# A decoder trunk's opening re-ordered: first w_mod tile loaded before x, seven bias units multiplied before the second K-tile, indicators of five of them made on GpSimd

## The chip, the cores and the metric

The kernel runs on one NeuronCore of a Trainium2 chip. The metric is the device time of one execution in microseconds (us), as the median of several runs. Engines are named as the profile names them: PE (TensorE, matmul), PEld (its weight loads), DVE (VectorE), ACT (ScalarE), POOL (GpSimd) and SP (SyncE, which here only issues DMAs).

## The reference, cut to what matters

```python
for l in range(DEPTH):                                  # DEPTH = 2, x is 512 x 2048, f32
    mod = silu(c) @ w_mod[l] + b_mod[l]                 # 2048 -> 3 * 2048
    shift, scale, gate = split(mod, 3)
    h = rmsnorm(x, norm_gain[l]) * (1 + scale) + shift
    proj = h @ w_in[l]                                  # 2048 -> 7504
    ...
    # group A: sparse attention; its logits get a bias from the positions alone:
    bias = rel_bias[t5_bucket(pos[q] - pos[k])]         # 32 buckets, 8 heads
    # group B: retention with rotary embedding
    x = x + gate * (concat([y_a, y_b]) @ w_out[l])
```

## The kernel before

Activations are kept transposed: model columns on partitions, the 512 tokens along the free axis. A K-tile is 128 of the 2048 model columns; there are 16, numbered 0 to 15 here. Every large product is made in three f32r passes (h-high by w-high, h-low by w-high, h-high by w-low), so each chunk of a weight (`wf`, from DRAM) is split into `wh` by ACT (L261) and `wl` by DVE (L268). A ring of three buffers each holds `wf`, `wh` and `wl`; SP issues the load of a chunk once the buffer of the chunk three before it is free.

`start()` is the opening. It is written out by hand, and each engine runs its part in the written order. It does, in this order:

- loads the constants `cst`, then the 16 K-tiles of x (256 KB each), then `w_mod`, laid out as one 128x2048 tile (1 MB) for each K-tile and each of scale and shift. Tile b=0 and b=1 make K-tile 0 ready, b=2 and 3 K-tile 1, and so on. The first four tiles come as two halves of 512 KB. Up to four tiles' loads stand ahead of their use;
- PE runs matmuls of zeros (`warm`) until there is work;
- `cb`, silu(c) spread over all partitions, is made by PE and copied by DVE; ACT squares each K-tile of x (L554), DVE adds the squares (`ssq`, L559), PE sums them over partitions (`row_sums`, L502), and `rstd_col` makes 1/rms and spreads it (`prb`, L484);
- `mod0_add()` multiplies one `w_mod` tile (or half) by `cb` and sums it on DVE (L349): 1.2 us for a half, 2.3 us for a tile. When the second tile of a K-tile is done, ACT makes h-high (L524) and DVE h-low (L530);
- `PLAN` lists the early chunks in the order in which PE takes them. `("S", i, kk)` is chunk i of the 336 columns of keys, values and indexer keys, `("E", i, a, b, kk)` group i of 256 columns over K-tiles a to b; a last number takes one K-tile of a two-tile chunk. Between these pieces `start()` puts a `mod0_add()` for every 4 units of PE cost, and one piece of the bias table for every 6.

The bias table is built in 32 units (j, q), each for 16 query rows against the first 128*(j+1) keys. A unit has four indicator tiles `ind` (128 thresholds against positions; ACT, Sign, L736), twelve matmuls with 32 output partitions each (L750, bf16), one evacuation `bt` (ACT, L755) and a store to DRAM, from which layer code reads it after 540 us. The units begin when K-tile 2 is ready, narrow ones first. PSUM has four banks under the tag `px` (units, E groups, broadcasts, warm-up) and four under `pj` (S and the rest).

The names `md`, `mp` are results of `mod0_add`, `hv` an f32 copy of h of which h-low is the rest, `part` the kept sums of an E group.

## Time and profile before

| | us |
|---|---|
| median of 3 runs (1915.17 to 1915.78) | 1915.41 |
| the profiled execution | 1916.6 |
| its span, first to last instruction | 1914.7 |
| PE busy in the span | 1888.6 (99%) |
| DVE busy | 1306.9 (68%) |
| ACT busy | 817.5 (43%) |
| POOL busy | 39.1 (2%) |

The span is what the trace shows; the profiled execution took 1.9 us more than it. PE's busy time counts the warm-up matmuls and matmuls at a lowered clock too. The page's row of the granted clock is 7 tenths in the first of 40 slices and 9 (90% or more) in the other 39.

### The profile page before, as it was taken

The page shows a single profiled execution, that of the slowest core. Times are in us where ns is not written, and L with a number is a line of the kernel's source. Part 1 is how long each engine was busy: PE and PEld are TensorE (multiplying, and loading weights), DVE is VectorE, ACT ScalarE, POOL GpSimd, SP SyncE. Part 2 cuts the span into 40 slices and gives each one's busy share as a digit, 9 for nine tenths or more (in the row PEclk, how much of TensorE's full clock was granted, in tenths as well). Part 3 has the DMA queues.
Part 4 walks back from the last instruction along what each step waited for, and adds up shares of the span by engine and source line. Part 5 has one row for each costly group of instructions (what it writes and reads, how often), then busy time and mean ns, then how long its engine had stood idle before and what let it go on. Part 6 is the DMA issues. An engine that isn't in the chain of part 4 may idle for free.

```text
span 1914.7 us, 24729 instructions
## 1 busy us (share of the span) xinstructions
PE 1888.6 (99%) x9136; PEld 1561.8 (82%) x9136; DVE 1306.9 (68%) x2261; ACT 817.5 (43%) x1498; POOL 39.1 (2%) x144
## 2 busy tenths in 40 slices
PE   7999999999999999999999999999999999999999
PEld 6777777888888888888888887888888888888887
DVE  7995699887867846877665579557775776564232
ACT  4666692355446522422233441244444563233111
POOL 0000000000000000100000000000000000000000
PEclk7999999999999999999999999999999999999999
DMA  9996233333352556689853223333324254553442
GB/s 369 334 307 214 88 91 108 99 110 100 121 176 89 176 176 231 235 286 309 307 162 110 78 77 99 107 92 110 99 88 125 85 190 140 180 184 121 143 139 103
DMA packets 166473, 304.44 MB, mean 159 GB/s; under 512 B 16336, under 2 KB 72144, under 8 KB 162768
## 3 DMA queue, kind: packets, MB, share of 16 engines
q1 hardware_dynamic: 166352, 302.86, 48.4%
q8 instruction: 72, 1.18, 0.2%
q14 instruction: 49, 0.40, 0.1%
HBM read 289.18 MB, written 13.63 MB: 158 GB/s over the span
## 4 chain that ended last, share of the span: by engine, by line
PE 83%; DVE 9%; ACT 4%; issue 2%; DMA 1%; SPq 0%; DVEq 0%; ACTq 0%
PE pj L322 20%; PE pj L324 20%; PE pj L323 20%; PE pj L328 5%; PE pj L329 5%; PE pj L330 5%; DVE wl L268 2%; DVE mw L349 1%; DVE iacc L872 1%; DVE iacc L857 1%; DVE m L871 1%; PE ptr L168 1%; PE plg L1068 1%; PE psc L949 1%; PE plg L1070 1%
## 5 line engine op out<-in xcount | busy, mean ns | idle before, releaser
L268 DVE TENSOR_TENSOR wl<-wf,wh 128x1024 fp32r<-128x1024 f32 (+3 forms) x309 | 366.5, 1187 | 436.8 <-ACT wh L261 423.7
L261 ACT ACTIVATE wh<-wf 128x1024 fp32r<-128x1024 f32 (+3 forms) x309 | 319.0, 1032 | 808.7 <-PE pj L323 591.0
L322 PE MATMUL pj<-h,wh 128*128 128x512 f32 x1280 | 502.6, 393 | 3.3 <-ACT h L524 2.5
L323 PE MATMUL pj<-h,wh 128*128 128x512 f32 x1280 | 500.9, 391 | 2.2 <-DVE h L530 2.2
L324 PE MATMUL pj<-h,wl 128*128 128x512 f32 x1280 | 500.5, 391 | 0.9 <-DVE wl L268 0.9
L322 PEld LDWEIGHTS pj<-h,wh 128*128 128x128 f32 x1280 | 240.7, 188 | 56.2 <-issue 2.9
L324 PEld LDWEIGHTS pj<-h,wl 128*128 128x128 f32 x1280 | 241.0, 188 | 52.3 <-DVE wl L268 2.7
L323 PEld LDWEIGHTS pj<-h,wh 128*128 128x128 f32 x1280 | 241.0, 188 | 51.6 <-DVE h L530 2.9
L328 PE MATMUL pj<-wh,h 128*128 128x512 f32 (+1 forms) x640 | 241.0, 377 | 2.9 <-DVE vm L887 2.6
L329 PE MATMUL pj<-wl,h 128*128 128x512 f32 (+1 forms) x640 | 240.2, 376 | 0.9 <-DVE wl L268 0.9
L330 PE MATMUL pj<-wh,h 128*128 128x512 f32 (+1 forms) x640 | 239.4, 376 | 0.0
L322 PE MATMUL pj<-y,wh 128*128 128x512 f32 x512 | 199.2, 389 | 0.0
L324 PE MATMUL pj<-y,wl 128*128 128x512 f32 x512 | 199.2, 389 | 0.0
L323 PE MATMUL pj<-y,wh 128*128 128x512 f32 x512 | 199.2, 389 | 0.0
L328 PEld LDWEIGHTS pj<-wh,h 128*128 128x128 f32 x640 | 120.2, 188 | 26.0 <-ACT wh L261 3.4
L329 PEld LDWEIGHTS pj<-wl,h 128*128 128x128 f32 x640 | 120.2, 188 | 20.6 <-DVE wl L268 1.4
L330 PEld LDWEIGHTS pj<-wh,h 128*128 128x128 f32 x640 | 119.7, 188 | 20.7 <-issue 0.4
L324 PEld LDWEIGHTS pj<-y,wl 128*128 128x128 f32 x512 | 96.1, 188 | 20.2
L322 PEld LDWEIGHTS pj<-y,wh 128*128 128x128 f32 x512 | 96.1, 188 | 20.1
L323 PEld LDWEIGHTS pj<-y,wh 128*128 128x128 f32 x512 | 96.1, 188 | 19.8
L349 DVE CUSTOM_DVE_ANT_0 mw<-mw,cb 128x1024 f32<-128x1024 f32 (+1 forms) x64 | 93.1, 1454 | 10.0 <-POOL mp L348 5.6
L349 DVE CUSTOM_DVE_ANT_0 mw<-mw,cb,mp 128x1024 f32<-128x1024 f32 x68 | 88.4, 1299 | 14.6 <-POOL md L348 7.6
(442 smaller groups left out, 2133.7 us busy)
## 6 DMA issues: line engine op xcount, KB each, us to landing
wf<-in_w_in_dram SPq DMA_DIRECT2D x155, 512.0 KB, 3.5
mw<-in_wmod_dram SPq DMA_DIRECT2D x136, 512.0 KB, 5.6
wf<-in_w_in_dram SPq DMA_DIRECT2D x136, 256.0 KB, 3.0
wf<-in_w_out_dram SPq DMA_DIRECT2D x64, 512.0 KB, 4.1
mw<-in_wmod_dram SPq DMA_DIRECT2D x28, 1024.0 KB, 7.8
dec<-in_decay_dram SPq DMA_DIRECT2D x32, 256.0 KB, 4.0
xT<-in_xt_dram SPq DMA_DIRECT2D x16, 256.0 KB, 5.3
bias<-bias_d SPq DMA_DIRECT2D x16, 256.0 KB, 4.3
```

Of the source, the lines that this page charges most:

```text
L168: nc.tensor.transpose(o, i, idn)
L261: act(h[:, :n], wf[i][:, :n], AF.Copy)
L268: tt(lo[:, :n], wf.pop(i)[:, :n], f(whl[i][:, :n]), op=OP.subtract)
L322: mm(g.ps[n], wh[:, o:o + P], ah, start=s0, stop=False)
L323: mm(g.ps[n], wh[:, o:o + P], al, start=False, stop=False)
L324: mm(g.ps[n], wl[:, o:o + P], ah, start=False, stop=s1)
L328: mm(q, ah[:, n * P:(n + 1) * P], wh[:, o:o + g.N], start=s0, stop=False)
L329: mm(q, ah[:, n * P:(n + 1) * P], wl[:, o:o + g.N], start=False, stop=False)
L330: mm(q, al[:, n * P:(n + 1) * P], wh[:, o:o + g.N], start=False, stop=s1)
L349: nc.vector.tensor_tensor_reduce(w[:, lo:hi], w[:, lo:hi], cb[:, lo:hi], scale=ng(l, k, 1) if q == 1 else 1.0, scalar=init, op0=OP.mult, o ...
L857: stt(a[:, :w], r[:, :w], L["WI"][:, c0:c0 + 1], a[:, :w], op0=OP.mult, op1=OP.add)
L871: nc.vector.max(m8, a[:, :w])
```

## The change

- SP loads the four halves of `w_mod` tiles 0 and 1 before x. `cst` is cut in two: 144 columns (identity, c) on SP's queue, the rest and the positions on ACT's queue.
- K-tile 0's four `mod0_add` stand among the squares of x instead of behind them. `cb` is copied by ACT and DVE in turns. K-tile 0's h is made by `make_h` in halves of 256 tokens straight from the PSUM of `prb`.
- The positions' conversion, the thresholds and doubled copies of the three bf16 parts of the bias differences (`be`, for indicators of +-0.5 rather than +-1) are made on POOL at the start.
- Units now run from the widest (j = 3, 512 keys) to the narrowest. Seven wide ones are multiplied in the opening: one after the tenth square, one after `prb`, five between K-tile 0's and K-tile 1's matmuls. `EU` says who makes their indicators: 1 is POOL (five units, 20 instructions of 128x512), 0 is ACT (two).
- `PLAN` takes S before E, and E group 1 whole after K-tile 1. `warm` numbers change.

```diff
-PLAN = [("E", 0, 0, 2, 0), ("E", 1, 0, 2, 0), ("S", 0, 0), ("E", 0, 0, 2, 1), ("E", 1, 0, 2, 1), ("S", 0, 1),
+PLAN = [("S", 0, 0), ("E", 0, 0, 2, 0), ("S", 0, 1), ("E", 0, 0, 2, 1), ("E", 1, 0, 2),
...
-WA, WS, WR = 36, 4, 8
+WA, WS, WL, WR = 24, 4, 20, 8
+
+EU = [1, 1, 0, 1, 0, 1, 1]
+EUK = (9,)
...
-    dma(cst, cst_d)
+    posi = gen.tile([P, T], I32, name="posi", tag="g")
+    dma(cst[:, :C_CAUS], cst_d[:, :C_CAUS])
+    adma(cst[:, C_CAUS:], cst_d[:, C_CAUS:])
+    adma(posi, bass.AP(tensor=positions.tensor, offset=positions.offset, ap=[[0, P], [1, T]]))
...
+        mod0_loads(4)
         for k in range(KT):
             load_x(k)
-        mod0_loads(2)
         ahead(1, 0)
-        mod0_loads(4)
+        mod0_loads(6)
...
+        get_ind(2)
         pss = psum.tile([P, T], F32, name="prs", tag="pj")
-        ssq, col = G("ssq"), 0
+        ssq, col, u = G("ssq"), 0, 0
+        mod0_add()
         for k in range(KT):
...
-            if k == 11:
+            if k < 3:
                 mod0_add()
+            if k in EUK:
+                flush()
+                begin(u)
+                u += 1
+        flush()
         col = row_sums(pss, ssq, col)
-        mod0_add()
-        rstd_col(pss, col, lambda: ahead(3, 0, 1))
         warm(WR)
-        mod0_add()
-        warm(WR, mpart["t"])
-        mod0_add()
-        xr0 = make_xr(0)
+        rstd_col(pss, col, lambda: ahead(3, 0, 1), "pj")
+        ahead(3, 1)
+        begin(u)
+        u += 1
+        make_h(0, 0, X[0], state["prb"])
         copy_rstd()
-        warm(WR // 2, mod_col(0, 0, 0))
+        ahead(3, 2)
+        flush()
+        get_ind(u + 3)
...
+            if kend == 2:
+                for u in range(u, len(EU)):
+                    begin(u)
+                    flush(1)
+                flush()
+                u = len(EU)
...
+    UNITS = [(j, q) for j in reversed(range(NB)) for q in range(8)]
...
+                if pool:
+                    nc.gpsimd.tensor_scalar(v, tab["pos"][:, :w], tab["pt"][:, col:col + 1], 0.5, op0=OP.is_lt, op1=OP.subtract)
+                else:
+                    act(v, tab["pos"][:, :w], AF.Sign, bias=tab["pt"][:, col:col + 1], scale=-1.0)
```

Three places in the engines' programs show what moves. First DVE, around the last sums of squares and 1/rms. An ISA row with `mw` is the product of one `mod0_add`, the ISA row behind it reads its sum out; `mb` is the bias of the modulation. Before, from K-tile 0's first product to its last:

```order
L349 ISA mw,mp<-mw,cb 128x1024
L349 ISA mp 128x1
L559 TENSOR_TENSOR ssq<-ssq,sq 128x512 x3
L349 ISA mw,md_88<-mw,cb,mp 128x1024
L349 ISA md_88 128x1
L474 TENSOR_REDUCE rcol<-prs 128x4
L478 RECIPROCAL rcol<-rcol 128x4
L349 ISA mw,mp<-mw,cb,cst 128x1024
L349 ISA mp 128x1
L349 ISA mw,md_88<-mw,cb,mp,cst 128x1024
L349 ISA md_88 128x1
L353 TENSOR_TENSOR md_88<-md_88,mb_90 128x2
```

After, from K-tile 0's third product to its h:

```order
L354 ISA mw,mp<-mw,cb,cst 128x1024
L354 ISA mp 128x1
L591 TENSOR_TENSOR ssq<-ssq,sq 128x512
L354 ISA mw,md_90<-mw,cb,mp,cst 128x1024
L354 ISA md_90 128x1
L358 TENSOR_TENSOR md_90<-md_90,mb_92 128x2
L591 TENSOR_TENSOR ssq<-ssq,sq 128x512 x9
L480 TENSOR_REDUCE rcol<-prs 128x4
L484 RECIPROCAL rcol<-rcol 128x4
L273 TENSOR_TENSOR wl<-wf,wh 128x672
L441 SCALAR_TENSOR_TENSOR u<-xT,md_90,prb 128x256 x2
L444 SCALAR_TENSOR_TENSOR h<-u,md_90,h 128x256 x2
```

K-tile 0's products now stand in front of the last nine sums of squares; between the sums and h only 1/rms and one split of weights are left.

Second ACT, from the square root in `rstd_col` to K-tile 1's h (the last `h` row of each piece). Before:

```order
L475 ACTIVATE rcol<-rcol,eps 128x4
L261 ACTIVATE wh<-wf 128x512
L490 ACTIVATE rstd<-prb 128x256 x2
L524 ACTIVATE h<-xT,md_88 128x512
L261 ACTIVATE wh<-wf 128x512
L261 ACTIVATE wh<-wf 128x672
L524 ACTIVATE h<-xT,md_88 128x512
```

After:

```order
L481 ACTIVATE rcol<-rcol,eps 128x4
L266 ACTIVATE wh<-wf 128x672
L442 ACTIVATE h<-u,md_90 128x256 x2
L496 ACTIVATE rstd<-prb 128x256 x2
L266 ACTIVATE wh<-wf 128x512
L794 ACTIVATE bt<-pb,top 128x512
L778 ACTIVATE ind<-pos,pt 128x512 x8
L530 ACTIVATE h<-xT,md_90 128x512
L794 ACTIVATE bt<-pb,top 128x512 x5
```

Eight indicators stand in front of K-tile 1's h, and five evacuations of units behind it.

Third SP, from the third chunk's load to the loads of groups E4 and E5 (`128x3x128`). Before:

```order
L253 DMA wf<-in_w_in_dram 128x2x256 x2
L669 DMA posi<-in_positions_dram 128x512
L381 DMA mw_408<-in_wmod_dram 128x2048
L381 DMA mw_435<-in_wmod_dram 128x2048
L381 DMA mw_441<-in_wmod_dram 128x2048
L381 DMA mw<-in_wmod_dram 128x2048
L253 DMA wf<-in_w_in_dram 128x3x128 x4
```

After:

```order
L258 DMA wf<-in_w_in_dram 128x2x256 x2
L797 DMA bias_d<-bt 128x512 x2
L386 DMA mw_480<-in_wmod_dram 128x2048
L386 DMA mw_487<-in_wmod_dram 128x2048
L386 DMA mw_493<-in_wmod_dram 128x2048
L386 DMA mw<-in_wmod_dram 128x2048
L797 DMA bias_d<-bt 128x512 x5
L258 DMA wf<-in_w_in_dram 128x3x128 x2
```

Seven stores of 256 KB now stand ahead of E4's weights.

## Rows read from the trace of the kernel before

**Rows 1.** The page: span, and busy time of each engine.

```profile
span 1914.7 us, 24729 instructions
PE 1888.6 (99%) x9136; PEld 1561.8 (82%) x9136; DVE 1306.9 (68%) x2261; ACT 817.5 (43%) x1498; POOL 39.1 (2%) x144
```

**Rows 2.** Busy time by stretch: the stretch, its length, busy us of PE, PEld, DVE, ACT and POOL (with the count of instructions), granted PE clock as a share, mean busy share of the DMA engines, GB/s.

```profile
0.00:28.47 28.47, 20.21 (x157) 19.04 (x157) 19.60 (x51) 15.73 (x28) 0.20 (x4) 0.76 0.97 357
28.47:39.71 11.24, 5.99 (x26) 4.23 (x26) 11.13 (x19) 2.05 (x3) 0.00 (x0) 0.90 1.03 409
39.71:46.27 6.56, 6.56 (x23) 5.55 (x24) 5.85 (x8) 4.59 (x8) 0.00 (x0) 0.65 1.03 378
```

**Rows 3.** PE in order of time: start, us, engine, line, operation, out<-in, form, count, and in brackets the idle time just before and what ended it.

```profile
10.74 1.00 PE L502 MATMUL prs<-cst,sq 128*128 128x1 f32 x8
...
21.24 1.87 PE L502 MATMUL prs<-cst,ssq 128*128 128x1 f32 x8 [4.96 <-DVE ssq L559]
...
28.47 0.51 PE L322 MATMUL pj<-h,wh 128*128 128x512 f32 x1 [0.31 <-ACT h L524]
...
34.69 0.32 PE L330 MATMUL pj<-wh,h 128*128 128x336 f32 x1
37.16 0.57 PE L322 MATMUL pj<-h,wh 128*128 128x512 f32 x1 [2.15 <-ACT h L524]
39.71 0.80 PE L323 MATMUL pj<-h,wh 128*128 128x512 f32 x1 [1.98 <-DVE h L530]
...
40.73 0.63 PE L322 MATMUL pj<-h,wh 128*128 128x512 f32 x1
41.15 0.63 PE L323 MATMUL pj<-h,wh 128*128 128x512 f32 x1
...
46.27 0.39 PE L322 MATMUL pj<-h,wh 128*128 128x512 f32 x1
46.50 0.39 PE L323 MATMUL pj<-h,wh 128*128 128x512 f32 x1
```

**Rows 4.** DVE in order of time, same columns.

```profile
17.75 1.23 DVE L349 CUSTOM_DVE_ANT_0 mw<-mw,cb 128x1024 f32<-128x1024 f32 x1 [2.21 <-DMA mw<-in_wmod_dram]
...
18.90 2.28 DVE L559 TENSOR_TENSOR ssq<-ssq,sq 128x512 f32<-128x512 f32 x3
...
23.14 0.18 DVE L474 TENSOR_REDUCE rcol<-prs 128x4 f32<-128x20 f32 x1 [0.76 <-PE prs L502]
23.69 0.18 DVE L478 RECIPROCAL rcol<-rcol 128x4 f32<-128x4 f32 x1 [0.36 <-ACT rcol L475]
...
26.55 0.75 DVE L516 TENSOR_TENSOR xT<-xT,prb 128x256 f32<-128x256 f32 x2
...
32.13 0.85 DVE L268 TENSOR_TENSOR wl<-wf,wh 128x672 fp32r<-128x672 f32 x1
...
36.09 0.16 DVE L353 TENSOR_TENSOR md<-md,mb 128x2 f32<-128x2 f32 x1
36.29 0.55 DVE L526 TENSOR_SCALAR hv<-xT,md 128x512 f32<-128x512 f32 x1
36.75 2.29 DVE L349 CUSTOM_DVE_ANT_0 mw<-mw,cb 128x2048 f32<-128x2048 f32 x1
...
38.96 0.69 DVE L530 TENSOR_TENSOR h<-hv,h 128x512 fp32r<-128x512 f32 x1
```

**Rows 5.** ACT in order of time, same columns.

```profile
16.54 0.63 ACT L554 ACTIVATE sq<-xT 128x512 f32<-128x512 f32 x1 [1.27 <-DMA xT<-in_xt_dram]
...
27.00 0.72 ACT L490 ACTIVATE rstd<-prb 128x256 f32<-128x256 f32 x2 [2.82 <-DVE xT L516]
...
36.29 0.81 ACT L524 ACTIVATE h<-xT,md 128x512 fp32r<-128x512 f32 x1 [6.18 <-DVE md L353]
...
48.06 0.85 ACT L261 ACTIVATE wh<-wf 128x768 fp32r<-128x768 f32 x1 [1.66 <-DMA wf<-in_w_in_dram]
...
59.23 1.06 ACT L261 ACTIVATE wh<-wf 128x1024 fp32r<-128x1024 f32 x1 [1.25 <-DMA wf<-in_w_in_dram]
```

**Rows 6.** SP's issues in order of time.

```profile
34.48 10.53 SPq L253 DMA_DIRECT2D wf<-in_w_in_dram  x4
```

**Rows 7.** PE around one unit of 512 keys: the matmul before it, its twelve, and the two after.

```profile
237.32 0.40 PE L324 MATMUL pj<-h,wl 128*128 128x512 f32 x1
237.65 0.83 PE L750 MATMUL pb<-ind,bd 128*32 128x512 bf16 x12
238.41 0.50 PE L849 MATMUL pdot<-kih,sa 128*128 128x512 f32 x1
238.75 0.39 PE L849 MATMUL pdot<-kih,sb 128*128 128x512 f32 x1
```

**Rows 8.** ACT's groups by shape: count | busy us, mean ns of one | idle before.

```profile
L736 ACT ACTIVATE ind<-pos,pt 128x512 bf16<-128x512 f32 x32 | 21.0, 752 | 0.2 <-PE pb L750 0.2
...
L755 ACT ACTIVATE bt<-pb,top 128x512 f32<-128x512 f32 x8 | 5.6, 704 | 0.0
```

**Rows 9.** POOL's widest groups by shape, same columns.

```profile
L807 POOL MEMSET iacc<- 128x384 f32 x2 | 0.8, 419 | 0.3 <-PE pki L168 0.3
L807 POOL MEMSET iacc<- 128x256 f32 x2 | 0.6, 312 | 0.4 <-issue 0.4
```

**Rows 10.** PE, a wait late in the early chunks.

```profile
138.54 0.50 PE L324 MATMUL pj<-h,wl 128*128 128x512 f32 x1 [0.74 <-DVE wl L268]
```

More of the change, by code (lines that the diff above doesn't have):

```diff
@@ L437, in make_h @@
             act(hh[:, c], u[:, c], AF.Identity, bias=mod_col(l, 0, k))
+        for c in HALF if isinstance(rstd, list) else [slice(0, T)]:
             stt(hl[:, c], u[:, c], mod_col(l, 0, k), f(hh[:, c]), op0=OP.add, op1=OP.subtract)
@@ L480, in rstd_col @@
         for c in HALF:
-            pb = PX("prb")[:, c]
+            pb = psum.tile([P, T], F32, name="prb", tag=tag)[:, c]
             for j in range(2):
@@ L545, in start, with get_ind, begin, flush @@
         act(cs, cst[:, C_C:C_C + KT], AF.Silu)
-        act(sm("dummy", 1), cs[:, :1], AF.Sqrt, bias=eps, scale=0.0)
-        next(bias)
+        pos_tables()
         pc = [bcast_c(i) for i in range(4)]
+        for i in range(4):
+            v = cb[:, i * T:(i + 1) * T]
+            if i % 2:
+                nc.vector.tensor_copy(v, pc[i])
+            else:
+                act(v, pc[i], AF.Copy)
+        act(onesr, ones, AF.Copy)
+        ind = {}
+        def get_ind(n):
+            for u in range(len(ind), min(n, len(EU))):
+                ind[u] = indicators(*UNITS[u], EU[u])
+        pend = []
+        def begin(u):
+            get_ind(u + 1)
+            pend.append(unit_mm(*UNITS[u], ind[u], EU[u]))
+        def flush(n=0):
+            while len(pend) > n:
+                unit_end(*pend.pop(0))
+        get_ind(2)
         pss = psum.tile([P, T], F32, name="prs", tag="pj")
-        ssq, col = G("ssq"), 0
+        ssq, col, u = G("ssq"), 0, 0
+        mod0_add()
         for k in range(KT):
@@ L621, in start @@
                 if "pos" not in flags:
-                    next(rot)
+                    flags.add("pos")
+                    next(bias)
                     for l in range(DEPTH):
@@ L667, in rot_tables @@
     def rot_tables():
[L668 to L674 removed]
+        pos = tab["pos"]
         ang, n, r = G("ang"), G("nn"), G("rr")
@@ L702, in rot_tables, with pos_tables @@
         yield 1.8, False
-    def bias_tables():
+    def pos_tables():
+        pos = G("pos")
+        nc.gpsimd.tensor_copy(pos, posi)
+        pt = sm("pt", P)
+        p4 = pos.rearrange("p (m l) -> p l m", l=4)
+        for tl in range(4):
+            nc.gpsimd.tensor_scalar(pt[32 * tl:32 * tl + 32, :], p4[32 * tl:32 * tl + 32, tl, :],
+                                    cst[32 * tl:32 * tl + 32, C_THR:C_THR + 1], None, op0=OP.subtract)
         top = sm("top", 1)
@@ L740, in bias_tables @@
[L740 to L762 removed]
+            b2 = sm(f"be{i}", 32, dt=BF)
@@ new lines, in pos_tables, with indicators @@
+            nc.gpsimd.tensor_scalar(b2, b, 2.0, None, op0=OP.mult)
+            twice.append(b2)
+        tab.update(pos=pos, pt=pt, top=top, parts=(parts, twice))
+    UNITS = [(j, q) for j in reversed(range(NB)) for q in range(8)]
+    def indicators(j, q, pool=False):
+        w = P * (j + 1)
+        ind = []
+        for i in range(2):
+            t = gen.tile([P, 2 * T], BF, name="ind", tag="g")
+            for u in range(2):
+                col = 32 * j + 4 * q + 2 * i + u
+                v = t[:, u * T:u * T + w]
+                if pool:
+                    nc.gpsimd.tensor_scalar(v, tab["pos"][:, :w], tab["pt"][:, col:col + 1], 0.5, op0=OP.is_lt, op1=OP.subtract)
+                else:
+                    act(v, tab["pos"][:, :w], AF.Sign, bias=tab["pt"][:, col:col + 1], scale=-1.0)
+                ind.append(v)
+        return ind
@@ new lines, in unit_mm, with unit_end, store @@
+    def unit_mm(j, q, ind, pool=False):
+        w = P * (j + 1)
+        ps = PX("pb")
+        for i in range(3):
+            for tau in range(4):
+                mm(ps[32 * tau:32 * tau + 32, :w], tab["parts"][pool][i], ind[tau],
+                   start=i == 0, stop=i == 2, tile_position=(0, 32 * tau))
+        return j, q, ps
+    def unit_end(j, q, ps):
+        w = P * (j + 1)
+        bt = G("bt")
+        act(bt[:, :w], ps[:, :w], AF.Identity, bias=tab["top"])
+        def store():
+            dma(bias_d[j].rearrange("(q r) h s -> q (r h) s", q=8)[q][:, :w], bt[:, :w])
+        stores.append(store)
@@ new lines, in bias_tables @@
+    def bias_tables():
+        todo = UNITS[len(EU):]
+        nxt = indicators(*todo[0])
+        yield 0.0, False
+        for u, (j, q) in enumerate(todo):
+            ind = nxt
+            nxt = indicators(*todo[u + 1]) if u + 1 < len(todo) else None
+            ps = unit_mm(j, q, ind)
+            if not st["i"]:
+                yield 0.0, False
+            unit_end(*ps)
+            if st["i"]:
+                while stores:
+                    stores.popleft()()
+            yield 0.0, False
```

71 lines of the change are left out of this document (9 added, 62 removed).

## The prediction

> **What bounds the kernel now.** I read the page first: PE is busy in 1888.6 of 1914.7 us [rows 1], so 26.1 us of idle time is all that better cover can win back over the whole span, unless PE's own work shrinks or is moved into that idle time. The stretches come next, since a share over the span mixes stages. Before 39.71 us PE is idle for 8.26 + 5.25 = 13.5 us, half of the whole, and from 39.71 to 46.27 it is busy throughout at a granted clock of 0.65 [rows 2]. The order of PE shows what these are. Its first real matmul starts at 28.47; after 24 of them it waits 2.15 us for K-tile 1's h-high and 1.98 us for its h-low; then matmuls start 0.42 us apart, where they start 0.23 apart at 46.27 [rows 3]. In the same stretch DVE is busy for 11.13 of 11.24 us [rows 2]: it makes K-tile 1's products, and its h-low ends at 39.65 [rows 4]. So the opening is bound by x and 1/rms up to 28 us and by DVE up to 39.7. From 46 us on PE is the bound but for small waits, the largest early one 0.74 us at 138 [rows 10]. What the change is worth is how much PE work it puts into the idle time, plus or minus what it moves the moment from which PE is full.
>
> **The change, step by step.**
>
> *Seven units into the gap.* With matmuls 0.23 us apart, the second matmul after the unit shown would have started at 237.32 + 0.46 = 237.78 without it; it started at 238.75. A unit of 512 keys thus takes 0.97 us of a full PE [rows 7]. There are 32 units before and after, and eight are that wide; seven leave the stretch in which PE is full: 7 x 0.97 = **6.8 us** gained, if they fit into idle time.
>
> *x and 1/rms.* Four halves of w_mod (2.10 MB) and the positions (0.26 MB) now go ahead of x. At 357 to 409 GB/s [rows 2] that is 5.8 to 6.6 us; I take 5.9. The last square started at 16.54 when its x landed [rows 5]; it would start at 22.4, end at 23.1, and its sum, 0.76 us as one of three in 2.28 [rows 4], at 23.8, where it was 21.2. The products no longer lie behind it: one of them had held the sums back until 18.9 [rows 4]; now they have the time in which x arrives. The row sums took 1.87 us after 4.96 us of idle time but 1.00 without it [rows 3]; with 28 warm-up matmuls beside them I take 1.0: 24.8. Reduce, root and reciprocal take 0.6 to the reciprocal's start [rows 4]; the split of S's weights stands next, 0.8 on ACT and 0.85 on DVE, then u in two halves, 0.75 by the like rows of `xT<-xT,prb` [rows 4], and half an h on ACT, between 0.36 (half of 0.72) and 0.81 [rows 5]. The first real matmul comes at about 27.8, 0.7 earlier than before.
>
> *K-tile 1.* Behind K-tile 0's h ACT has 0.72 for rstd and 0.63 for E0's weights, so E0's `wl` ends on DVE at about 30.2. Four halves at 1.23, x times rstd at 0.6 and the bias make `md` ready at 36.0; it was 36.09 [rows 4]. What was won on the way is spent on E0's split, which now waits for ACT. So K-tile 1 is ready when it was: h-high near 37.0, h-low near 39.6. Bounds: 2 us earlier if x comes at the upper rate and ACT's order costs nothing, 3 later if the row sums still take 1.87 and x comes at the lower one.
>
> *Does PE have the room?* Its idle time there was 5.25 us, and the six E1 matmuls that leave give 1.4 more: 6.6, against six units at 5.8 (the seventh lies ahead of 28 us). One thing squeezes them. E0 holds two of the four `px` banks, and the evacuations of the last five units stand behind K-tile 1's h on ACT. The fourth of the seven can be multiplied at once, the next only when a bank is evacuated after 37.1, at 0.70 each [rows 8]; the last ends at about 40.3, and K-tile 1's S starts then, 0.6 later than its first long run did (39.71). Then S, E0 and the whole of E1 are 30 matmuls, 5.9 us at the full clock: 46.2, against 46.27. That needs the clock to hold. In the kernel before, it did not after 4.1 us of waits: ten matmuls cost 0.2 more each, 2.0 us. I take no loss, since units now stand among the waits, and 2.5 as the other end.
>
> *The indicators.* POOL has no such row. Its memsets took 0.312 at 256 columns and 0.419 at 384 [rows 9], which carried on gives 0.53 at 512; the upper end is ACT's 0.752 for the same indicator [rows 8]. Twenty are 10.6 to 15.0 us. They can start at about 8 us, when the positions and thresholds are there, and the last is needed at about 39: they are hidden, and would be up to 1.5 us each. The Trainium skill (GPSIMD Engine Reference, "Elementwise — side-by-side cycle accounting") has 769 ns measured for 512 elements, an estimate of 15.4 us for twenty; no run here shows it. ACT's eight indicators at 0.64 to 0.752 take 5.1 to 6.0 us from about 30.3, so they end just as `md` comes at 36.0: at worst 0.4 late.
>
> *The queue.* Seven stores of 256 KB, 1.84 MB, now stand ahead of E4's weights on SP; at 378 GB/s [rows 2] that is 4.8 us of traffic in a stretch where the DMA engines are full. Those weights were issued from 34.48 [rows 6] and landed at 48.06 [rows 5]; now they may land between 50 and 53. PE wants E4 at 51.7 (24 matmuls after 46.27) and its third pass 0.45 later, and both splits need 1.8 before that. So PE loses 0 to 2.7 us there; E6's weights, which landed at 59.23 [rows 5], have about as much room and do not add to it. I take **1.0 us** lost.
>
> *The wait at 138.* Units on the way there are now wide where they were narrow, so PE comes later against DVE: the 0.74 us [rows 10] should go; the other end is that it stays. I take **0.7 us** gained.
>
> *Sum.* -6.8 - 0.7 + 1.0 = -6.5 us. The profiled execution took 1916.6 (its span 1914.7 and 1.9 around it), so 1910.1; the median of the runs is 1.2 below it, so **1908.9 us**.
>
> **Rivals.**
>
> *DVE and POOL hold each other up (slower).* DVE's products, sums and splits read two tiles each, and POOL's twenty instructions now run beside them for the first time; before, POOL did not work in this stretch at all (0.20 and 0.00 us in [rows 2]), so no row speaks for or against. If DVE stood still for each, 15.0 us would fall on the chain that makes 1/rms and K-tile 1. DVE had 2.2 us of waiting for DMA to give [rows 4]; the rest, about 12.5, moves the whole kernel: 1921. It decides the sign from 6.5 us on, about 0.43 us for each of the twenty beyond the slack, and costs over 0.2% from 10.3 us beyond the forecast. The Trainium skill (SBUF — State Buffer, "Who interferes with whom") states just this: a DVE instruction with two SBUF inputs contends with a GpSimd instruction that reads SBUF, and the one that comes second is blocked for the whole of the other. By that rule the time would lie towards 1921; no run here shows it yet. I give the full form 8 in 100 and a half of it (1912 to 1919) 10, since one POOL instruction can also pass while DVE waits for x or reads PSUM.
>
> *The queue binds.* E4's and E6's weights come at the late end: 1.7 to 4 us more, 1911 to 1913. For it: full DMA engines in [rows 2] and ACT already waiting 1.66 and 1.25 for these two [rows 5]. Against it: the issue of E4's weights used to stand far ahead of their use. 12 in 100.
>
> *The clock falls among the units or x comes late.* 2 to 3 us: 1911 to 1912. For it: the clock did fall between 37 and 40 before [rows 3]. 10 in 100.
>
> *It wins more.* K-tile 1 comes 2 us earlier and the weights in time: 1906. For it: DVE has less to do between x and h. 15 in 100.
>
> **How the numbers follow.** The forecast (1907 to 1911.5) has 45 in 100, the rivals 8, 10, 12, 10 and 15. 0.2% of 1915.4 is 3.8 us, about what a measurement can tell from no change: faster means below 1911.6, slower above 1919.2. Faster are the forecast, the larger win and some of the queue's and clock's cases: 0.68. Slower is the full rival of DVE and POOL: 0.08. The rest, 0.24, is within 0.2%. The range reaches from the larger win with a little of the 138 us stretch besides (1904.5) to the queue's worst end and the start of the half rival (1915); the DVE and POOL cases above that and a small tail below are left out, about 2 in 10.
>
> **What would show it.** Right: `ssq`'s last sum ends near 23.8, the first S matmul near 28, six units lie between 27 and 40.5 on PE, K-tile 1's h-low ends at 39 to 40, and E2 starts near 46 at the full clock with seven units done. The twenty POOL instructions take 0.5 to 0.8 us and end before 30. The wait at 138 is gone. Wrong: DVE's products in the opening take clearly over 1.23 us or its sums over 0.7 (POOL in its way); POOL's are over 1.5 us, so that PE waits for `ind`; PE waits for `wl` of E4 or E6 while ACT waits for `wf`; matmuls 0.42 us apart after K-tile 1's h.

## The result: 14 us slower

The changed kernel took 1929.76 us (median of 4 runs, 1929.52 to 1930.28), the kernel before 1915.60 beside it: a ratio of 1.007, 95% interval 1.0052 to 1.0087, so 14.2 us slower. The prediction was 1908.9 in a range of 1904.5 to 1915.0. Measured once more beside the runs below (e8), the changed kernel took 1931.25 against 1916.92 (1.0075, 1.0059 to 1.0090).

**The profile after.** The page: span and busy time of each engine, which answers [rows 1].

```profile
span 1928.1 us, 24722 instructions
PE 1893.1 (98%) x9124; PEld 1565.0 (81%) x9124; DVE 1306.2 (68%) x2254; ACT 806.9 (42%) x1480; POOL 91.7 (5%) x172
```

Of the 13.4 us that the span grew, PE's work is 4.5 and PE's idle time 8.9; POOL works 52.6 us more. Busy time by stretch, the first three stretches as in [rows 2]:

```profile
0.00:28.47 28.47, 20.20 (x135) 18.40 (x135) 18.18 (x42) 14.47 (x24) 21.47 (x20) 0.74 0.96 342
28.47:39.71 11.24, 10.96 (x77) 7.71 (x77) 7.83 (x15) 7.89 (x16) 11.24 (x6) 0.74 0.84 300
39.71:46.27 6.56, 1.04 (x14) 0.34 (x14) 6.49 (x9) 3.26 (x5) 6.56 (x3) 0.87 0.97 375
46.27:60.00 13.73, 5.00 (x22) 0.99 (x21) 3.23 (x4) 0.69 (x1) 12.45 (x6) 0.50 0.50 195
```

The second stretch looks like what the change wanted: PE busy for 10.96 of 11.24 us (before: 5.99). But half of that, up to 34.05, is row sums, warm-ups, broadcasts and one unit, all of them ahead of the first real matmul, which started at 28.47 before. Behind it PE works for 1.04 of 6.56 and 5.00 of 13.73 us. From 46.27 on DVE, ACT and the DMA engines have little to do too, and POOL works without a break. The waits of PE from 10 to 70 us (total us, times, longest), and POOL's row for the indicators in order of time:

```profile
PE pb L787 <- POOL ind L776: 10.6, 6, 3.1
PE prs L508 <- ACT sq L584: 7.1, 2, 5.9
PE pb L787 <- ACT bt L794: 4.0, 1, 4.0
```

```profile
13.01 45.71 POOL L776 TENSOR_SCALAR ind<-pos,pt 128x512 bf16<-128x512 f32 x20
L776 POOL TENSOR_SCALAR ind<-pos,pt x20: 1987/1992/3582, 13.0 to 56.7; 128x512 bf16<-128x512 f32 x20
```

POOL's twenty indicators run from 13.01 to 58.72, 2.29 us each on average; the second row is their summary (ns: least/median/most). PE in order of time, which answers [rows 3]:

```profile
15.04 1.87 PE L508 MATMUL prs<-cst,sq 128*128 128x1 f32 x8 [5.95 <-ACT sq L584]
...
25.94 2.29 PE L473 MATMUL pw<-wz 128*128 128x128 bf16 x20
28.02 1.81 PE L508 MATMUL prs<-cst,ssq 128*128 128x1 f32 x8
...
34.05 0.53 PE L333 MATMUL pj<-wh,h 128*128 128x336 f32 x1
...
43.38 0.83 PE L787 MATMUL pb<-ind,bd 128*32 128x512 bf16 x12 [3.95 <-ACT bt L794]
...
47.53 0.58 PE L787 MATMUL pb<-ind,be 128*32 128x512 bf16 x1 [3.10 <-POOL ind L776]
50.89 1.44 PE L787 MATMUL pb<-ind,be 128*32 128x512 bf16 x9 [2.78 <-POOL ind L776]
...
58.77 1.44 PE L787 MATMUL pb<-ind,be 128*32 128x512 bf16 x9 [1.39 <-POOL ind L776]
60.14 0.65 PE L333 MATMUL pj<-wh,h 128*128 128x336 f32 x1
```

PE takes its work in the written order, so K-tile 1's matmuls, ready at 45.7, stand behind units 6 and 7 until 60.14. SP stands behind the same units: the five stores hold its queue for 18 us, and E4's weights are issued only then (SP's issues, [rows 6]):

```profile
43.36 17.98 SPq L797 DMA_DIRECT2D bias_d<-bt  x5
62.27 0.92 SPq L258 DMA_DIRECT2D wf<-in_w_in_dram  x2
```

DVE, which answers [rows 4]:

```profile
15.49 0.69 DVE L591 TENSOR_TENSOR ssq<-ssq,sq 128x512 f32<-128x512 f32 x1
16.09 1.63 DVE L354 CUSTOM_DVE_ANT_0 mw<-mw,cb,mp 128x1024 f32<-128x1024 f32 x1
...
17.84 8.49 DVE L591 TENSOR_TENSOR ssq<-ssq,sq 128x512 f32<-128x512 f32 x9
29.87 0.18 DVE L480 TENSOR_REDUCE rcol<-prs 128x4 f32<-128x20 f32 x1 [3.54 <-PE prs L508]
...
41.75 0.16 DVE L358 TENSOR_TENSOR md<-md,mb 128x2 f32<-128x2 f32 x1
41.95 0.93 DVE L532 TENSOR_SCALAR hv<-xT,md 128x512 f32<-128x512 f32 x1
...
45.01 0.68 DVE L536 TENSOR_TENSOR h<-hv,h 128x512 fp32r<-128x512 f32 x1
```

Some of DVE's instructions now take longer: the second half of a `mod0_add` 1.63 (1.28 to 1.35 before), `hv` 0.93 (0.55, [rows 4]). The wait at 138 us [rows 10] is gone.

### The profile page after: what moved, and what is told of

It reads as the page before. It is cut to its first block, busy times and chain, and to the rows that moved or that the text cites. A ratio compares the mean times of both kernels' runs of the same rounds, so it can differ in the third digit from the quotient of the medians.

```text
span 1928.1 us, 24722 instructions
## 1 busy us (share of the span) xinstructions
PE 1893.1 (98%) x9124; PEld 1565.0 (81%) x9124; DVE 1306.2 (68%) x2254; ACT 806.9 (42%) x1480; POOL 91.7 (5%) x172
## 4 chain that ended last, share of the span: by engine, by line
PE 87%; DVE 6%; ACT 3%; POOL 2%; issue 1%; DMA 1%; SPq 0%; ACTq 0%; DVEq 0%
PE pj L327 20%; PE pj L329 20%; PE pj L328 20%; PE pj L333 5%; PE pj L334 5%; PE pj L335 5%; POOL ind L776 2%; DVE wl L273 1%; DVE iacc L924 1%; DVE m L923 1%; DVE iacc L909 1%; PE pb L787 1%; DMA xT<-in_xt_dram 1%; PE ptr L171 1%; PE pdot L901 1%
## 5 line engine op out<-in xcount | busy, mean ns | idle before, releaser
L273 DVE TENSOR_TENSOR wl<-wf,wh 128x1024 fp32r<-128x1024 f32 (+2 forms) x309 | 366.2, 1185 | 457.8 <-ACT wh L266 444.5
L266 ACT ACTIVATE wh<-wf 128x1024 fp32r<-128x1024 f32 (+2 forms) x309 | 318.7, 1032 | 806.8 <-PE pj L328 596.2
```

Source lines behind the costliest of these rows:

```text
L266: act(h[:, :n], wf[i][:, :n], AF.Copy)
L273: tt(lo[:, :n], wf.pop(i)[:, :n], f(whl[i][:, :n]), op=OP.subtract)
```

## The experiments

All beside the kernel before on the same chip. "Reduce" is the start of DVE's reduction for 1/rms, "h-low" the end of K-tile 1's h-low, both in us from the start of the span.

| run | us | before | ratio, 95% interval | reduce | h-low |
|---|---|---|---|---|---|
| kernel before | | | | 23.1 | 39.7 |
| changed kernel | 1929.76 | 1915.60 | 1.0070 (1.0052-1.0087) | 29.9 | 45.7 |
| e1 four units | 1918.93 | 1916.96 | 1.0012 (1.0002-1.0021) | 29.5 | 44.4 |
| e2 no units | 1921.28 | 1916.96 | 1.0024 (1.0014-1.0033) | 27.6 | 42.5 |
| e3 forms on POOL | 1926.09 | 1916.96 | one run | 29.5 | 46.0 |
| e4 all on ACT | 1924.52 | 1916.96 | 1.0040 (1.0025-1.0055) | 32.4 | 47.2 |
| e5 no units, PE kept busy | 1923.08 | 1916.92 | 1.0029 (1.0019-1.0038) | 28.0 | 42.8 |
| e6 x first, four units on ACT | 1918.21 | 1916.92 | 1.0005 (0.9996-1.0014) | 24.5 | 41.1 |
| e7 POOL's tiles unread | 1930.51 | 1916.92 | 1.0067 (1.0054-1.0081) | 27.7 | 43.6 |
| e8 changed kernel again | 1931.25 | 1916.92 | 1.0075 (1.0059-1.0090) | 29.4 | 45.2 |
| e9 POOL's tile apart | 1948.13 | 1917.14 | 1.0158 (1.0144-1.0172) | 27.9 | 43.8 |
| e10 POOL copies | 1919.50 | 1917.14 | 1.0011 (1.0002-1.0020) | 29.5 | 44.3 |
| e11 K-tile 1 ahead of 1/rms | 1919.64 | 1917.14 | 1.0010 (1.0001-1.0020) | 28.2 | 40.6 |
| e12 e11 + three units on ACT | 1916.46 | 1917.14 | 0.9996 (0.9987-1.0005) | 28.6 | 40.9 |
| e13 before + h-low first | 1917.30 | 1917.65 | 1.0000 (0.9990-1.0009) | 22.7 | 37.3 |
| e14 e12 + h-low first | 1918.14 | 1917.65 | 1.0002 (0.9993-1.0011) | 28.9 | 39.4 |
| e15 e11 + h-low first | 1920.04 | 1917.65 | 1.0015 (1.0006-1.0024) | 28.1 | 38.6 |
| e16 x first, no units | 1919.26 | 1917.65 | 1.0011 (1.0002-1.0020) | 24.6 | 41.2 |
| e17 opening of before, three units | 1916.57 | 1917.08 | 0.9994 (0.9985-1.0003) | 23.8 | 40.6 |
| e19 the same, four units | 1914.65 | 1917.08 | 0.9989 (0.9980-0.9998) | 23.9 | 40.7 |

### Who makes the indicators, and for how many units

Theory after the result: one POOL indicator costs over three times what was assumed, and the units in PE's order wait for it. Rival: the order of the loads alone makes the opening late.

e1, two units on POOL and two on ACT:

```diff
-EU = [1, 1, 0, 1, 0, 1, 1]
+EU = [1, 1, 0, 0]
```

> The changed kernel with four early units in place of seven (EU = 1,1,0,0): POOL makes 8 indicators, all used ahead of K-tile 0's h or beside it, and none stands between K-tile 0's and K-tile 1's matmuls; the other three units follow later as before. If POOL's price is the cause (2.0 to 2.3 us for an instruction, so that PE waits for units 5 and 6 until 59.7 us): PE's wait for POOL goes, S of K-tile 1 starts when its h-low is there, about 45.7 us against 60.2, and the time falls by 14.5 less three units at 0.97: about 1918 us. If DVE held up by POOL is the cause, the delay lies ahead of 31 us, where POOL still works, and the time stays above 1925.

e2, none:

```diff
-EU = [1, 1, 0, 1, 0, 1, 1]
-EUK = (9,)
+EU = []
+EUK = ()
```

> The changed kernel with no early units (no indicators on POOL at all, all 32 units later, widest first); the order of loads, squares, sums and K-tile 0's h as changed. If w_mod ahead of x by itself makes K-tile 1 late: its h-low still comes near 45 us (39.65 before) and the time is 1915.6 + 5 to 6, about 1921. If POOL's instructions had held DVE up in this stretch, the sums of squares take 0.7 us each as before, K-tile 1's h-low comes near 40 and the time is within 1 us of before, 1915 to 1917.

e4, seven, all on ACT (`EU = [0] * 7`):

> The changed kernel with all seven units' indicators on ACT (EU all 0), 28 at 0.64 us = 18 us more on ACT, eight of them ahead of the squares of x and twelve ahead of K-tile 1's h. If POOL's price is the cause, taking POOL out wins even though ACT is now in the way: the squares end about 4.5 us later, K-tile 1's h-high near 50, and PE never waits for POOL: 1917 to 1922 us. If the price of the indicators does not matter and the order of the opening alone is at fault, it stays near 1928 or gets worse.

Three POOL units fewer took 12.3 us off (e1 against e8), as the theory had it. Without any, 4.3 us of loss remain (e2): that is the most that the rival can claim, and e16 below takes some of it away again. Where it arises is in e2's PE and DVE rows; with POOL out of the way the sums of squares end at 24.3:

```profile
25.78 1.81 PE L508 MATMUL prs<-cst,ssq 128*128 128x1 f32 x8
```

```profile
27.63 0.18 DVE L480 TENSOR_REDUCE rcol<-prs 128x4 f32<-128x20 f32 x1 [3.34 <-PE prs L508]
```

The last row sums start 1.5 us behind the last sum, since twenty warm-up matmuls at the low clock stand ahead of them, and take 1.81 us. e4 is no way out and missed its 1917 to 1922: eight indicators wait on ACT for POOL's `pt` and hold the first square until 16.10.

e3 has POOL make its five units in five forms, four instructions each (the branches written shorter here):

```diff
+if q == 0: nc.gpsimd.tensor_scalar(v, p, s, 0.5, op0=OP.is_lt, op1=OP.subtract)
+elif q == 1: nc.gpsimd.tensor_scalar(v, p, s, None, op0=OP.is_lt)
+elif q == 3: nc.gpsimd.tensor_scalar(v, p, 0.001, None, op0=OP.mult)
+elif q == 5: nc.gpsimd.tensor_scalar(v, p, 100.0, 0.5, op0=OP.is_lt, op1=OP.subtract)
+else: nc.gpsimd.tensor_scalar(v, p, 0.001, 0.25, op0=OP.mult, op1=OP.subtract)
```

> The changed kernel with each of the five POOL units in another form of the same 128x512 instruction (f32 in, bf16 out), four each, so that the bias table holds other numbers: in order of time (compare with a column, subtract 0.5) as changed; compare with a column alone; multiply by a constant alone; compare with a constant, subtract 0.5; multiply by a constant, subtract a constant. If the price is that of elements and memory ports, all take about 2.0 us when DVE stands still. If the second operation is a second pass in software, the forms with one take near 1.0 to 1.3; if the comparison is what costs, the multiplications take near 0.6, as the cast of the positions did (0.61).

The lines' summaries (ns: least/median/most), and from the groups POOL's conversion of the positions (busy us, mean ns):

```profile
L778 POOL TENSOR_SCALAR ind<-pos,pt x4: 1989/2230/2832, 12.7 to 20.0; 128x512 bf16<-128x512 f32 x4
L780 POOL TENSOR_SCALAR ind<-pos,pt x4: 1556/1734/1912, 21.9 to 27.3; 128x512 bf16<-128x512 f32 x4
L782 POOL TENSOR_SCALAR ind<-pos x4: 1484/1486/1488, 28.8 to 33.2; 128x512 bf16<-128x512 f32 x4
L786 POOL TENSOR_SCALAR ind<-pos x4: 1916/2451/3903, 43.8 to 52.6; 128x512 bf16<-128x512 f32 x4
```

```profile
L737 POOL CAST pos<-posi 128x512 f32<-128x512 int32 x1 | 0.6, 612 | 6.4 <-DMA posi<-in_positions_dram 6.4
```

Neither the comparison nor the operand in a column is dear: a comparison alone takes 1.56 at least and a multiplication alone 1.48, a second operation makes it 1.92 to 1.99 (1.92 in the fourth form too, whose row is not shown), and a conversion alone takes 0.61.

### Is it POOL's price? (e10, e8)

e10 lets POOL copy the positions in place of comparing them; e8 is the changed kernel once more.

```diff
-nc.gpsimd.tensor_scalar(v, tab["pos"][:, :w], tab["pt"][:, col:col + 1], 0.5, op0=OP.is_lt, op1=OP.subtract)
+nc.gpsimd.tensor_copy(v, tab["pos"][:, :w])
```

> The changed kernel with GpSimd's twenty indicators replaced by plain copies of the positions to bfloat16 (the bias tables then hold other numbers: it shows times alone). GpSimd's copy of 512 elements took 0.61 us where its comparison took 1.99, so that it lies in the 0.53 to 0.75 us that the prediction had assumed. Theory (the price of one GpSimd indicator was the step that failed most, and the opening's other delays make up the rest): GpSimd done by 30 us, PE waits nowhere for it, seven units are done before K-tile 1's h-low at 44 to 45.5, and the time is 1913 to 1919: 1917 + 4.4 for the order of loads + 1.4 to 3 for units ahead of the row sums - 6.8. Rival (banks, ScalarE's evictions or the two engines' contention hold the units up whatever the price): 1924 or more.

> The changed kernel itself, on this chip, so that the three others have it beside them: 14 us above the kernel before, as in its own comparison.

e10's POOL row, and its PE in order of time:

```profile
12.46 18.27 POOL L776 CAST ind<-pos 128x512 bf16<-128x512 f32 x20
```

```profile
42.42 1.47 PE L787 MATMUL pb<-ind,bd 128*32 128x512 bf16 x12 [3.41 <-ACT bt L794]
43.65 2.80 PE L787 MATMUL pb<-ind,be 128*32 128x512 bf16 x24
46.38 0.65 PE L333 MATMUL pj<-wh,h 128*128 128x336 f32 x1
```

At 0.91 us each on average (0.61 at least, 1.60 at most) POOL is done by 30.7, PE waits for no indicator, and the time falls from 14.3 to 2.4 us above before. So 12.0 us, good to some 3 by the two intervals, are the price of POOL's instruction, with what a longer POOL takes from DVE in it (h-low 45.2 against 44.3). The expected 1913 to 1919 was missed by 0.5. Even so the seven units give back only 2.0 us against e2 (2.5 by the ratios), where 6.8 were expected: unit 5 waits 3.41 us for a PSUM bank, whose evacuation stands behind K-tile 1's h on ACT, and units 5 to 7 run at the low clock, 1.2 to 1.4 us each where unit 3 took 0.66.

### What POOL takes from the others (e7, e9)

e7 is e2 with twenty POOL indicators that nobody reads; e9 writes them all into a tile of its own.

```diff
+for q in range(5):
+    indicators(3, q, True)
```

> The kernel without units in the opening, in which GpSimd makes twenty indicator tiles of 128x512 in its place of the changed kernel, and nobody reads them: what they cost is then only what GpSimd takes from the other engines. Theory (VectorE and GpSimd hold each other up): sums of squares at up to 1.07 us in place of 0.69, the halves of K-tile 1's x*w_mod at 1.6 in place of 1.25, K-tile 1's h-low ends near 45 in place of 42.5, and the time is 2 to 3 us above that of the kernel without units. Rival (in the changed kernel VectorE was late for another reason, the units on TensorE and ScalarE among them): VectorE's rows and the time as without units, 42.5.

```diff
+own = arena.tile([P, 8 * T], BF, name="own", tag="HP7")
+for c in range(20):
+    nc.gpsimd.tensor_scalar(own[:, :T], tab["pos"], tab["pt"][:, 96 + c:97 + c], 0.5, op0=OP.is_lt, op1=OP.subtract)
```

> As the run with twenty GpSimd tiles that nobody reads, but all twenty are written over each other into a tile of their own, which no other work needs before about 100 us, instead of into the ring of buffers that ScalarE's parts and the other tiles of 128x512 use. In the run before it ScalarE waited 8.8 us in two pieces at 61 and 65 us for a buffer that GpSimd was still writing. Theory (most of the 9 us which the unread tiles cost is this wait for buffers; what the two engines take from each other is about 1 us on K-tile 1's h-low): h-low ends near 43.5, no wait for GpSimd's tiles, the time 1 to 2 us above the kernel without units (1922 to 1923). Rival (VectorE held up by GpSimd all the way to 65 us is what costs): the time stays at 1928 to 1931.

e7's time, 9.3 us further above before than e2's, was not what either theory named. ACT's waits in e7, then in e9, from 28 to 140 us:

```profile
ACT part L1256 <- POOL ind L779: 8.8, 2, 5.5
```

```profile
ACT wh L266 <- DMA wf<-in_w_in_dram: 22.7, 1, 22.7
```

In e7 the tiles come from the ring of buffers that ACT's `part` uses too, and ACT waits 8.8 us for buffers that POOL still writes. e9 was to take that away and failed: the place I chose is one that a `w_mod` tile uses next, so SP's queue stood until POOL had done (65.9), and 31 us were lost. Its time says nothing of contention. What both say is K-tile 1's h-low, which no buffer held up: 43.6 and 43.8 against 42.5. So POOL's neighbourhood costs DVE's chain 1.1 to 1.3 us. POOL itself needs more than in the changed kernel, 52.4 and 53.2 us for the twenty in place of 45.7, with DVE at work for longer beside it.

### The rest of the opening (e5, e11, e16)

e5 is e2 with PE kept at work while x arrives, e11 has K-tile 1's first two halves ahead of 1/rms, e16 loads x first in the changed kernel's code, without units, K-tile 0's products back in their old places (its edit stands with e6's, below).

```diff
-WA, WS, WL, WR = 24, 4, 20, 8
+WA, WS, WL, WR = 24, 10, 4, 8      # e5
+warm(80)                           # e5, ahead of the squares
```

> The kernel without units in the opening (of which the row sums ran at a granted clock of 0.50, 1.87 us each, after 6.7 us without work on TensorE), with one more change: 80 more warm-up matmuls ahead of the squares of x, and of the ones among the squares 10, 10, 10 and 4 in place of 4, 4, 4 and 20. Theory A (x behind K-tile 0's weights leaves TensorE without work, the clock falls, and 20 slow warm-ups stand ahead of the last row sums): the row sums take about 1.0 us at the full clock, the last ones start with the end of the last sum of squares (24.3), 1/rms comes about 2.5 us earlier, K-tile 1's h-low ends at about 40 in place of 42.5, and the time falls by 2 to 3 us against the kernel without units. Rival (the chain of DVE from the sums of squares to K-tile 1's h-low is what lasts, whatever TensorE's clock is): h-low within 0.7 us of 42.5 and the time the same.

```diff
-WA, WS, WL, WR = 24, 4, 20, 8
+WA, WS, WL, WR = 24, 4, 4, 8       # e11
         flush()
+        mod0_add()
+        mod0_add()
         col = row_sums(pss, ssq, col)
```

> The kernel without units, with two edits: K-tile 1's first two halves of w_mod are multiplied by VectorE ahead of the reduction of 1/rms (where it idled for 3.3 us), not behind K-tile 0's h, and 4 warm-ups in place of 20 ahead of the last row sums. Theory (K-tile 1's h came 2.8 us later than in the kernel before because VectorE's chain for it started only with 1/rms, which came 4.5 us later): h-low of K-tile 1 ends at 39.2 to 40.2 in place of 42.5, and the time is 2 to 3 us below the kernel without units (1918 to 1919.5). Rival (K-tile 1's halves have not landed by then: the transfers set the time): VectorE waits for them ahead of 1/rms, h-low at 42 or later, the time the same or longer.

> The changed kernel's code with x loaded first and K-tile 0's products in their old places, without units: what is left of the rewrite is the rest (c's broadcasts ahead of the squares, positions loaded at the start, the wide units first among those that come later). Theory (w_mod ahead of x costs the 4.4 us): 1/rms within 1.5 us of before, h-low of K-tile 1 at 39.6 to 41.2, the time 0 to 2 us above the kernel before. Rival (the rest of the rewrite costs it): 3 us or more above.

e5 decided nothing: PE still had 3.30 us without work before the row sums, which ran at the low clock (1.87), and its third x came 1.2 us late. e11: h-low at 40.6 in place of 42.5, though DVE waited 1.11 us for the second half of the tile; the loss fell from 4.3 to 2.5 us (by the ratios from 0.24 to 0.10%). So K-tile 1 was late because its products stand on DVE behind 1/rms; e11's other edit, fewer warm-ups, is not the cause, since the reduction for 1/rms came later there than in e2 (28.2 against 27.6). e16 came out as its theory had it: about 1.6 of e2's 4.3 us come not from the order of the loads but from the rest of the rewrite; 1/rms is 1.4 us late there.

### Is K-tile 1's h-low the end of the opening? (e13, e14, e15)

In every kernel it stands behind K-tile 2's first product (2.29 us, [rows 4]). The edit, in the kernel before, e12 and e11:

```diff
         def mod_step():
+            if 1 in hgen:
+                next(hgen.pop(1))
+                st["have"] = 2
```

> The kernel before with one edit: K-tile 1's h-low stands on VectorE ahead of K-tile 2's first product (2.29 us), behind which TensorE waited 1.98 us for it. Theory (K-tile 1's h-low is what sets the end of the opening): it ends at 37.8 to 38.1 in place of 39.65, the wait of the third pass falls under 0.4 us, and the time falls by 1 to 2 us. Rival (K-tile 2, which comes 0.7 us later, or the transfers set it): the wait is gone and the time is within 0.5 us of the kernel before.

> The kernel without units and with K-tile 1's halves ahead of 1/rms, with the same edit: h-low at about 38.5 in place of 40.6. Theory: 1 to 2 us below that kernel's 1919.6. Rival: the same time.

> The kernel with three units on ScalarE and K-tile 1's halves ahead of 1/rms, with the same edit. Theory: 1 to 2 us below that kernel's 1916.5, that is 1914.5 to 1915.5, 2 us below the kernel before. Rival: 1916 to 1917.

h-low came 2.3 us earlier in e13, 1.5 in e14 and 2.0 in e15, and no gain shows: by the medians beside before -0.35 us in e13, +1.2 in e14 against e12 and -0.1 in e15 against e11. One such difference is good to some 2 us; the three together speak against a gain of 1 to 2. e13's PE in order of time:

```profile
37.38 0.50 PE L323 MATMUL pj<-h,wh 128*128 128x512 f32 x1 [0.23 <-DVE h L530]
43.30 0.50 PE L324 MATMUL pj<-h,wl 128*128 128x512 f32 x1 [0.81 <-DVE wl L268]
51.27 0.50 PE L324 MATMUL pj<-h,wl 128*128 128x512 f32 x1 [1.54 <-DVE wl L268]
```

The 1.98 us wait of [rows 3] came back as waits for `wl`, although PE's granted clock stayed at 1.00 from 39.71 to 46.27, where it was 0.65 before. The rows are those of the fastest of e13's eleven executions; even there PE reaches the same matmul only 0.83 us earlier than before (56.34 against 57.17), and 0.5 of that was there at the reduction. The busy times of e13 from 46.27 show why: PE has 1.88 us idle there, DVE 0.16.

```profile
46.27:60.00 13.73, 11.85 (x60) 8.62 (x59) 13.57 (x22) 10.73 (x21) 0.00 (x0) 1.00 1.01 350
```

So the theory is not borne out: K-tile 1's h-low alone does not set the end. The rows point to DVE's whole work, which has no room up to 60 us in e13, and up to 46.27 in e14 and e15 (6.53 of 6.56 us from 39.71), where PE waits 2.26 and 2.25 us for a `wl`; that was not tested by itself.

### What a unit is worth (e6, e12, e17, e19)

e6 is e16 with four units; e12 is e11 with three, `pt` on DVE. e17 and e19 keep the opening of the kernel before (x, `cb`, K-tile 0) and put three and four units into it, positions and `pt` on POOL. All make their indicators on ACT. e17 and e19 also take over the changed kernel's `PLAN` and its order of units, and leave out two groups of warm-ups.

e6, against the changed kernel (e16 is the same with `EU = []`):

```diff
-WA, WS, WL, WR = 24, 4, 20, 8
+WA, WS, WL, WR = 36, 4, 40, 8
-EU = [1, 1, 0, 1, 0, 1, 1]
+EU = [0, 0, 0, 0]
...
-        mod0_loads(4)
         for k in range(KT):
             load_x(k)
+        mod0_loads(2)
         ahead(1, 0)
-        mod0_loads(6)
+        mod0_loads(4)
...
-            if k < 3:
+            if k == 11:
                 mod0_add()
...
+        get_ind(2)
         col = row_sums(pss, ssq, col)
...
+        begin(0)
+        begin(1)
```

> x loaded first as in the kernel before, with K-tile 0's adds of w_mod in their old places among the squares and around 1/rms; four units of 512 keys in the opening, their sixteen indicators on ScalarE (eight behind the squares while it waits for 1/rms, eight between 1/rms and K-tile 1's h); no indicators on GpSimd. Theory (a unit is worth its 0.97 us on TensorE wherever it fills the wait for K-tile 1's h, if nothing that K-tile 1's h waits for is made later): K-tile 1's h-low at 39 to 40.5, all four units done by 40.5, the time 3 to 4 us below the kernel before. Rival (K-tile 1's h depends on ScalarE too, and the indicators push it back): h-low at 42 or later, the time within 2 us of the kernel before.

e12, against e11:

```diff
-EU = []
-EUK = ()
+EU = [0, 0, 0]
+EUK = (0,)
...
-        get_ind(2)
+        get_ind(1)
...
+        get_ind(2)
         mod0_add()
         mod0_add()
         col = row_sums(pss, ssq, col)
```

> The run before it with three units in the opening, their twelve indicators on ScalarE in stretches where it waited: four while the first tile of x is on its way (pt by VectorE, to have it in time), four behind the squares, four behind K-tile 0's h. Theory (a unit that fills TensorE's wait for K-tile 1's h is worth 0.97 us when nothing is put behind GpSimd): h-low of K-tile 1 as there (39.2 to 40.5), the time 2.5 to 3 us below it, 1915 to 1917, the same as or up to 2 us below the kernel before. Rival (the work that the units filled later is missing there, and TensorE waits there instead): no more than 1 us below it.

e17, what it adds to the opening of the kernel before; e19 has four zeros and `get_ind(4)`:

```diff
+EU = [0, 0, 0]
...
         rstd_col(pss, col, lambda: ahead(3, 0, 1), "pj")
+        get_ind(1)
...
         copy_rstd()
+        begin(0)
...
         next(hgen.pop(0))
...
+        flush()
+        get_ind(3)
```

> The kernel before with its own opening (x first, c's broadcasts among the squares, K-tile 0's products in their places), positions loaded behind the first halves of w_mod, their cast and pt on GpSimd, and three units of 512 keys whose twelve indicators ScalarE makes in its waits: four behind 1/rms, eight behind K-tile 0's h. The row's tiles are taken in the order S, E0, S, E0, E1 as in the changed kernel. Theory (a unit is worth its 0.97 us wherever no engine that is full makes anything for it): 1/rms and K-tile 1's h-low within 0.5 us of before (23.1 and 39.65), the time 2 to 3 us below the kernel before. Rival (VectorE sets the opening's end, and what TensorE does in its waits is not worth more than a part): 0 to 1 us below.

> The same with a fourth unit, whose four indicators (2.5 us) stand on ScalarE between K-tile 0's h and K-tile 1's: they end about 1.3 us past the place where K-tile 1's h could start. Theory: as the run with three, within 0.7 us of it, since what the unit gives back K-tile 1's h loses. Rival (a unit is worth it even so): 0.7 to 1 us below it.

Six pairs differ by units alone, or nearly so. By the ratios three units took 0.14% off e11 (2.7 us, 0.9 each: e12) and 0.13% off e15 (2.5 us, 0.8 each: e14), the fourth 0.05% off e17 (1 us: e19), four 0.06% off e16 (1.1 us, 0.3 each: e6) and 0.12% off e2 (2.3 us, 0.6 each, two of them by POOL: e1), seven with a cheap POOL 0.13% off e2 (2.5 us, 0.4 each: e10). The medians beside before say 3.2, 1.9, 1.9, 0.3, 2.4 and 2.0 us. With intervals of +-0.09% each, such a difference is good to some 2 us: the pairs cannot tell 0.97 us for a unit from half of it.

Of the expectations, e12's theory held. e6's did not: h-low came at 41.1 and the time stayed 1.3 us above before. In e17 the rival held (0.5 us below by the medians, 1.1 by the ratio); 1/rms was 0.7 us late and h-low 1.0. e19's two theories lie too close together to be told apart (1.0 us below e17 by the ratios, 1.9 by the medians). e19 is the only version faster than before, by 2.1 us, its interval just below 1; among nineteen comparisons one such interval can come by chance. Its idle time does not explain it: in e19 PE had 3.93 us idle from 28.47 to 39.71 where the kernel before had 5.25 [rows 2], but the slower e17 had 3.41.

## Why the prediction was wrong, step by step

**The account.** Forecast and measurement are 20.7 us apart (-6.5 and +14.2). About 12.0 are POOL's price (e8 against e10), 4.3 the opening that comes late even without units (e2), and 4.8 what seven units fail to give back with a cheap POOL (2.0 of 6.8, e10).

**The indicators** are the step that failed first of all. It took POOL's memsets [rows 9] and ACT's indicator [rows 8] as bounds, 0.53 to 0.752, and wrote that twenty are hidden and "would be up to 1.5 us each". A memset reads no tile and computes nothing, and ACT is another engine: the nearest rows were no bounds at all. Measured: a median of 1.99, 2.29 in the mean beside DVE, 45.7 us in all in place of 10.6 to 15.0. The start was wrong as well, 13.01 for 8: the positions landed at 6.8, and `pt` and `be` kept POOL until 13.0. With the last one needed at 39, that leaves 1.3 us each to hide in, not 1.5. The Trainium skill's 769 ns for 512 elements (GPSIMD Engine Reference, "Elementwise — side-by-side cycle accounting"), which the page gives for the best case of a tight loop, was as far off: none of POOL's indicators in the changed kernel took under 1.98 us. The place where the cover ends was computed, so the loss follows: units 6 and 7 wait until 58.7, and with them PE's order and SP's stores.

**x and 1/rms.** The arrival held: last sum at 24.3 without POOL (e2) for 23.8. The row sums did not: 1.81 for 1.0, and 1.5 us of warm-up ahead of them (e2), which the step had counted as help for the clock. In the changed kernel the first unit stands there as well, at the low clock (22.81 to 24.21), and beside POOL the sums end at 26.3 (25.8 in e7). First real matmul at 30.7 in e2 and 34.05 after, for 27.8.

**K-tile 1.** 39.6 expected, with "3 later" as the far bound; e2 gave 42.5, just that bound, and the changed kernel 45.7. DVE's chain for it starts with 1/rms, so 1/rms passes its delay on; e11 shows it by taking two halves out of the chain.

**Seven units into the gap, room on PE.** Whether a unit in the gap is worth its 0.97 us is not settled: 0.8 to 1 in e12, e14 and e19, 0.3 in e6, each good to some 2 us for the whole pair. For seven it failed even with a cheap POOL: 2.0 us for 6.8 (e10). The bank wait was foreseen, but its end at 37.1; it came at 42.4, as K-tile 1 was late. The clock's other end, 2.5 us, was nearer than the zero that was taken: units 5 to 7 of e10 took 3.96 us, three at unit 3's 0.66 would be 1.98.

**The queue, the wait at 138.** With POOL cheap (e10), the weights came late, as feared: ACT waited 2.59 us for those that it split at 56.61, four indicators and an evacuation of sums (`part`) stand behind that split on ACT, and PE waited 1.62 us for the evacuation, where 1.0 was taken:

```profile
60.44 0.50 PE L327 MATMUL pj<-h,wh 128*128 128x512 f32 x1 [1.62 <-ACT part L1253]
```

The wait at 138 is gone, as said.

**The rivals.** DVE and POOL do hold each other up, but by a fraction. The sums of squares of the changed kernel, eleven beside a POOL that works without a break (ns: least/median/most), and below them those of e2, where POOL makes none:

```profile
L591 DVE TENSOR_TENSOR ssq<-ssq,sq x11: 685/693/1073, 13.7 to 25.6; 128x512 f32<-128x512 f32 x11
L591 DVE TENSOR_TENSOR ssq<-ssq,sq x11: 685/692/693, 13.0 to 23.6; 128x512 f32<-128x512 f32 x11
```

The rule that the second is blocked for the whole of the other (Trainium skill, SBUF — State Buffer, "Who interferes with whom") would hold a sum up by as much as POOL's 2 us; here most lose nothing and the worst 0.38. It cost DVE's chain 1.1 to 1.3 us (e7, e9), far under the rival's half. POOL lost more, 0.3 us on each in the mean (2.29 for 1.99), 6 us in all; with it gone POOL would still end at 52.8. That the result lies on the slower side, as this rival had it, is therefore luck. Its cause is the price itself, which the prediction had among its signs of being wrong ("over 1.5 us, so that PE waits for `ind`") but not among its rivals, so without a chance. Two sums in this rival are off and decide nothing: 15.0 less 2.2 is 12.8, not 12.5, and 6.5 us over twenty are 0.33 each beyond the slack (0.43 counts the slack in).

**What stays open.** What a unit is worth, to better than half, and whether e6's 1.1 us for four and e12's 2.7 for three differ at all; which of e16's edits costs its 1.6 us; what sets the end of the opening, if not K-tile 1's h-low.
